# Output projection as seven block products instead of plain tiles, with the first MLP pairs reordered, in a one-core decoder layer

## The chip, the cores and the metric

One Trainium2 chip, one core. The metric is the device time of one execution in microseconds. A profile is one profiled execution; its span runs from the first to the last instruction. The engines are TensorE (PE, with its weight loads PEld), VectorE (DVE), ScalarE (ACT), GpSimd (POOL) and SyncE (SP), which issues the DMAs.

## What is computed

One layer of a hybrid decoder, x of 1024 positions by 1024 features, float32. The part around the change:

```python
merged = (jax.nn.sigmoid(g_a) * (y_att @ w_oa[l])
          + jax.nn.sigmoid(g_b) * (y_sgu @ w_ob[l]))
x = x + merged @ w_out[l]
x = x + conv_gated_mlp(rmsnorm(x, ffn_norm[l]), w_up[l], conv_w[l], conv_b[l], w_down[l])
```

The gates g_a and g_b are columns of an input projection of the normed x; y_att is a sliding-window attention, y_sgu a chunked spatial gating unit. The MLP projects up to twice 2816 columns (22 pairs of a gate tile and a value tile of 128 columns), convolves each over three positions, multiplies silu(gate) with value, and projects down.

## The kernel before

Everything is transposed: features on the 128 partitions, positions along the free axis. TensorE runs in a reduced float format (fp32r), so every operand is split into a high part (ACT, `copy_hi`, line 87) and a low part (the difference, on POOL or DVE), and a product is three matmuls: high by high, high by low, low by high (`mm3`, lines 89 to 93).

The big products of the gates, the up projection and the down projection are already done as seven block products instead of eight: both operands are cut into 2 x 2 blocks, and with A for weights, B for the right side, S and T for sums of their blocks,

```
M1 = A11 B11   M2 = A12 B21   M3 = S4 B22   M4 = A22 T4   M5 = S1 T1   M6 = S2 T2   M7 = S3 T3
```

are combined into the four result blocks. `Blocks.prod` (line 1028) is one such product for one column tile: 4 blocks of 128 x 3 = 12 matmuls of 128x128 by 128x512. The sums of the weights (S) are made ahead for the up projection: `sums_load` and `sums_step` load a unit into one of two `ls` buffers, DVE makes two differences, and the unit goes back to DRAM. `sums_step` is called from `gate_pair` (twice for c > 1) and from the branches.

Stages, in order: attention, the spatial gating unit, the gates (8 `gate_pair`s of 7 products), the branches (16 jobs of 24 matmuls: one tile of y_att or y_sgu products, times 1 + tanh of its gate), the output projection, the up projection (22 pairs), the down projection.

Branches and output projection are **jobs**. `run_jobs` takes them in order: a job's matmuls, then the weight load of the job four ahead, then the weight split of the job two ahead, then the rest of the job (what is done with its result). Weights are loaded into three raw buffers and split into two high (`wh`) and two low (`wl`) buffers. The order in which instructions are issued in the text is the order on every engine (manual schedule), DMAs on SP included.

The output projection before is eight jobs (`out_tile`, in the order D_ORDER) of 8 x 2 x 3 = 48 matmuls: one tile of 128 features over all 1024 positions, in a PSUM tile of two banks. Behind each, DVE adds half of it to x (line 1285), scales by the norm's weight and by the first norm's row factor to h (line 1287), x goes to DRAM, and h is split into the blocks B11, T1, B21, B22, T3 of the up projection, while T2 and T4 stay raw (`raw2`, `raw4`) until `first_pair`. Squares for the second norm are summed in `sq2` (lines 1304 to 1307).

PSUM has eight banks of 128x512 floats: two pools, psA and psC, of two tiles of two banks each. `PS` hands out their tiles in turn.

`first_pair` is the first pair of the up projection: zg with halves g0 and g1, zv with halves v0 and v1. Its products in order: A11·B11 into v1, A12·B21 into g0, S1·T1 into g1, S3·T3 into v0, S4·B22 into g1, S2·T2 into v1, the norm's column sums (`ssq_cols`, line 1354), A22·T4 into v0. The copies between them move a half to SBUF (x1, x7, u2). `fast_pair` does the others; for the second pair it has `rms`, which brings the row factor onto all partitions (line 138) and scales the first pair.

Of the kernel before, what the change touches and what calls it, by code (L numbers as in the profile page):

```python
# [41 lines left out]
def body(ctx, tc, nc, a):  # L42
# [654 lines left out]
    def job_load(i):  # L697
        if i < len(jobs):
            src, nk, _ = jobs[i]
            job_w[i] = wload(src, "wj", nk) if nk else first_left()  # L700
            if not nk:
                next(job_w[i])

    def job_split(i):
        if i < len(jobs):
            nk = jobs[i][1]
            if nk:
                job_w[i] = wsplit(job_w[i], "wj", nk)
            else:
                for _ in job_w[i]:  # L710
                    pass
# [107 lines left out]
    def v_end():  # L819
# [14 lines left out]
        psC = psum["C"].__enter__()  # L834
# [93 lines left out]
    class Left:  # L928
# [75 lines left out]
        def split_r(self, n=0):  # L1004
            if "AX" not in pools:
                pools["AX"] = Y("AX")
# [43 lines left out]
    sums = {"load": 0, "make": 0}  # L1050

    def sums_load():

        i = sums["load"]
        if i < NPAIR:
            x = pools["ls"].tile([128, 3, 4, 128], F, tag="ls", name=nm("ls"), bufs=2)
            nc.sync.dma_start(x[:, 0], a["wup"][2 * i][:, 0:4])
            nc.sync.dma_start(x[:, 1:3], a["wup"][2 * i + 1].rearrange("p (b k) m -> p b k m", b=2))
            sums[i] = x
            sums["load"] += 1  # L1060

    def sums_step():

        i = sums["make"]
        if i < NPAIR:
            sums_load()
            x = sums.pop(i)
            sub(nc.vector, x[:, 0], x[:, 0], x[:, 1])
            sub(nc.vector, x[:, 1], x[:, 1], x[:, 2], ALU.add)
            t = pools["dr"].tile([128, 2, 4, 128], F, tag=f"sum{i}", name=f"sum{i}")  # L1070
            nc.sync.dma_start(t, x[:, 0:2])
            pools.setdefault("sum", {})[i] = t
# [22 lines left out]
    def gates_close():  # L1095
# [3 lines left out]
        pools["mg_cm"] = tc.tile_pool(name="mg", bufs=1)  # L1099
        pools["mg"] = pools["mg_cm"].__enter__()  # L1100

    def gate_pair(c, prev):
# [16 lines left out]
        if c > 1:  # L1119
            sums_step()  # L1120
# [15 lines left out]
        if c > 1:  # L1136
            sums_step()
# [14 lines left out]
        gate_out(("a", c), q.zv)  # L1152
        q.prod(q.g1, "S4", "B22", more=True)
# [35 lines left out]
    B_ORDER = [(br, c + e) for c in range(0, 8, 2) for br in "ba" for e in (0, 1)]  # L1189
    ms = {}  # L1190
# [655 lines left out]
```

## Time and profile before

| | |
|---|---|
| median of 3 runs | 1194.13 us (1193.82 to 1194.5) |
| the profiled execution | 1193.8 us, span 1192.1 us, granted clock 1.0 |
| PE busy | 1180.0 us, 99% of the span, 5890 matmuls |
| DVE, ACT, POOL busy | 877.8, 541.8, 567.4 us |
| DMA queue of the core | 190.26 MB, 45.9% of 16 engines |
| branches | about 380 to 467.6 us of the span |
| output projection | 467.6 to 555 us |
| first MLP pair | from 555 us |

How to read the rows that follow: a group of instructions has its line, engine, operation, out<-in by the program's names, partitions x elements, a count, then busy us and mean ns of one, then the idle time of that engine ahead of them and what ended it. A row of the timeline begins with start and length in us. A row of the waits has who waited for whom, us in total, times, and the longest. A row of a stretch has for each engine its busy us and in brackets the instructions, then the granted PE clock, the DMA share and GB/s.

### The profile page before, as it was taken

What the parts mean: (1) busy time and instruction counts of PE and PEld (TensorE: products, weight loads), DVE (VectorE), ACT (ScalarE), POOL (GpSimd) and SP (SyncE); (2) the same over time, 40 slices, a digit from 0 to 9 for tenths busy, and PEclk for the clock granted to TensorE, in tenths of its full rate; (3) what the DMA queues carried; (4) which work ended last, traced back from release to release, by engine and by line L of the source; (5) the groups of instructions that cost most, each with busy time, mean ns of one, the idle gap of its engine ahead of it and who ended that gap; (6) DMA issues with size and microseconds to landing.
All of it is one profiled execution on the core that took longest, in us unless ns stands there. A gap on an engine that the chain in (4) does not pass through costs nothing.

```text
span 1192.1 us, 15888 instructions
## 1 busy us (share of the span) xinstructions
PE 1180.0 (99%) x5890; PEld 1000.9 (84%) x5890; DVE 877.8 (74%) x1028; ACT 541.8 (45%) x832; POOL 567.4 (48%) x364
## 2 busy tenths in 40 slices
PE   8999999999999999999999999999999999999998
PEld 8989989988888888888888888888888888888887
DVE  7798975745638565668897788878788798865674
ACT  8555567644335222234544444444444445434331
POOL 2367685487768222343756575656657551000000
PEclk9999999999999999999999999999999999999999
DMA  7110133037786997342143342423333258966471
GB/s 272 35 54 19 54 136 130 5 130 260 245 315 212 347 327 278 125 165 100 54 142 108 104 143 98 148 91 124 108 131 124 89 209 290 373 230 194 151 233 67
DMA packets 79134, 191.27 MB, mean 160 GB/s; under 512 B 8913, under 2 KB 9169, under 8 KB 79057
## 3 DMA queue, kind: packets, MB, share of 16 engines
q1 hardware_dynamic: 79056, 190.26, 45.9%
q8 instruction: 46, 0.75, 0.3%
q14 instruction: 32, 0.25, 0.1%
HBM read 139.63 MB, written 50.59 MB: 160 GB/s over the span
## 4 chain that ended last, share of the span: by engine, by line
PE 89%; DVE 4%; POOL 1%; issue 1%; ACT 0%; POOLq 0%; DVEq 0%; ACTq 0%
PE pz L1028 48%; PE pd L1672 10%; PE pdy L1672 8%; PE px L93 2%; PE px L92 2%; PE po L93 2%; PE po L92 2%; PE po L91 2%; PE px L91 2%; PE pvs L91 1%; PE pvs L92 1%; PE pvs L93 1%; DVE ya L529 1%; PE pq L91 1%; PE pq L93 1%; PE pq L92 1%
## 5 line engine op out<-in xcount | busy, mean ns | idle before, releaser
L1028 PE MATMUL pz<-T,qh 128*128 128x512 f32 x472 | 145.6, 390 | 0.0
L988 POOL TENSOR_TENSOR pl<-lp,ph 128x1024 fp32r<-128x1024 f32 x30 | 72.5, 2418 | 83.5 <-ACT ph L87 83.3
L1028 PE MATMUL pz<-B,ph 128*128 128x512 f32 x352 | 109.1, 391 | 0.0
L1028 PEld LDWEIGHTS pz<-T,qh 128*128 128x128 f32 x472 | 88.5, 188 | 18.6 <-ACT u L879 0.3
L1028 PE MATMUL pz<-T,ql 128*128 128x512 f32 x236 | 91.8, 389 | 0.0
L108 POOL TENSOR_TENSOR wjl<-wj,wjh 128x512 fp32r<-128x512 f32 (+1 forms) x24 | 40.6, 1692 | 95.8 <-ACT wjh L87 95.8
L988 POOL TENSOR_TENSOR ql<-lq,qh 128x1024 fp32r<-128x1024 f32 x30 | 76.9, 2565 | 9.1 <-ACT qh L87 9.1
L1028 PEld LDWEIGHTS pz<-B,ph 128*128 128x128 f32 x352 | 65.3, 188 | 15.0 <-ACT x L1519 1.8
L1044 DVE TENSOR_TENSOR pz<-pz,rstd_b 128x1024 f32<-128x1024 f32 x60 | 73.9, 1232 | 4.2 <-ACT rstd_b L141 2.1
L988 POOL TENSOR_TENSOR s3l<-s,s3h 128x512 fp32r<-128x512 f32 x29 | 39.8, 1373 | 69.7 <-ACT s3h L87 69.7
L1028 PE MATMUL pz<-T,s3h 128*128 128x512 f32 x232 | 71.4, 389 | 0.0
L1028 PE MATMUL pz<-B,pl 128*128 128x512 f32 x176 | 68.6, 390 | 0.0
L1672 PE MATMUL pd<-bl,ah 128*128 128x512 f32 x176 | 68.5, 389 | 0.0
L1672 PE MATMUL pd<-bh,ah 128*128 128x512 f32 x176 | 68.5, 389 | 0.0
L1672 PE MATMUL pd<-bh,al 128*128 128x512 f32 x176 | 68.5, 389 | 0.0
L1028 PE MATMUL pz<-T,AX 128*128 128x512 f32 x264 | 63.4, 389 | 0.0
L1028 PE MATMUL pz<-B,AX 128*128 128x512 f32 x264 | 63.4, 389 | 0.0
L1028 PEld LDWEIGHTS pz<-T,AX 128*128 128x128 f32 x264 | 49.6, 188 | 10.3
L1028 PEld LDWEIGHTS pz<-B,AX 128*128 128x128 f32 x264 | 49.6, 188 | 10.3
L1378 DVE SCALAR_TENSOR_TENSOR tg<-pz,cp,tg 128x1023 f32<-128x1023 f32 (+1 forms) x44 | 56.2, 1278 | 0.8
L1378 DVE SCALAR_TENSOR_TENSOR tv<-pz,cp,tv 128x1023 f32<-128x1023 f32 (+1 forms) x44 | 56.2, 1277 | 0.8
L988 POOL TENSOR_TENSOR AX<-lr,AX 128x1024 fp32r<-128x1024 f32 x22 | 53.7, 2440 | 5.1 <-ACT AX L87 5.1
(342 smaller groups left out, 3511.8 us busy)
## 6 DMA issues: line engine op xcount, KB each, us to landing
ls<-wup SPq DMA_DIRECT2D x22, 512.0 KB, 5.3
sum<-ls SPq DMA_DIRECT2D x22, 512.0 KB, 5.3
lp<-wup SPq DMA_DIRECT2D x22, 512.0 KB, 3.6
ra<-wdown SPq DMA_DIRECT2D x44, 256.0 KB, 4.6
b<-T SPq DMA_DIRECT2D x44, 256.0 KB, 3.8
B<-tv SPq DMA_DIRECT2D x33, 256.0 KB, 2.0
T<-tt SPq DMA_DIRECT2D x33, 256.0 KB, 2.0
b<-B SPq DMA_DIRECT2D x33, 256.0 KB, 3.1
```

The source lines that it names most:

```text
L91: nc.tensor.matmul(out, wh, mh, start=first, stop=False, **kw)
L92: nc.tensor.matmul(out, wh, ml, start=False, stop=False, **kw)
L93: nc.tensor.matmul(out, wl, mh, start=False, stop=last, **kw)
L108: nc.gpsimd.tensor_tensor(l[:, :nk, :], r[:, :nk, :], h[:, :nk, :].bitcast(F), op=ALU.subtract)
L529: nc.vector.tensor_tensor(ya[r, 2 * half:2 * half + 2, b * 128:(b + 1) * 128], p[r, g], o[r], op=ALU.add)
L988: nc.gpsimd.tensor_tensor(l, r, h.bitcast(F), op=ALU.subtract)
L1028: nc.tensor.matmul(o, p[:, k, :], y[:, q, k, :], start=not more and k == 0 and j == 0, stop=k == 3 and j == 2, skip_group_check=True)
L1044: nc.vector.tensor_tensor(z, z, rstd_b, op=ALU.mult)
L1378: nc.vector.scalar_tensor_tensor(t[:, j:], p[:, 0:1024 - j], cw[:, ci, 2 - j:3 - j], t[:, j:], op0=ALU.mult, op1=ALU.add)
L1672: nc.tensor.matmul(o[d], p[:, k - k0, m], q[:, k - k0, :], start=new and k == 0 and j == 0, stop=k == HK - 1 and j == 2, skip_group_check= ...
```

## The change

The output projection becomes fourteen jobs (`out_group`), two for each of seven block products, 24 matmuls each (4 tiles d x 2 blocks k x 3). merged is kept raw in `mraw`, and its sums T are formed in place: three differences in `m_done` as the branches end, the rest and the splits in `m_prep`, two groups ahead. The sums of w_out come from eight new units of `sums_step` (four DVE operations each), in DRAM as `d_so`; `gate_pair` calls `sums_step` three times instead of two (twice for c = 1). The branches' order pairs tile c with c + 4.

The eight PSUM banks hold X (four halves, psC) and Yb (four halves, psA) through the whole projection. M1 goes to X, is copied to Yb (`copies`), M2 onto Yb gives C11; M6 onto X, M7 into Yb, M5 onto X gives C22, M3 onto X gives C12, M4 onto Yb gives C21. Each end (`end_c11` and so on) adds half the block to x, stores it, and makes the up projection's blocks with h = x times the norm's weight alone; the row factor is now applied in `rms` whole. Each end yields ahead of its last quarter, d = 3, and there `run_jobs` puts the weight split of the job two ahead.

`first_pair` takes PSUM tiles from psC and runs A11·B11 into v1, S3·T3 into v0, S1·T1 into g1, A12·B21 into g0, S4·B22 into g1, S2·T2 into v1, A22·T4 into v0. The squares of C21 and C12 are added within it. The norm's column sums move into the second pair, where the products now go A11·B11, column sums, A12·B21, row factors, S1·T1, S3·T3.

The diff, cut to what matters (`first_left` also changes its form, and `job_load`, `job_split` call functions kept in the job):

```diff
@@ run_jobs
             m = jobs[i][2](job_w.pop(i))
             next(m)
             job_load(i + 4)
+            if len(jobs[i]) > 3:
+                next(m)
             job_split(i + 2)
             for _ in m:
                 pass
@@ sums
+    UNITS = [("o", 0), ("o", 1)]
+    for c in range(6):
+        UNITS += [("u", 2 * c), ("o", c + 2), ("u", 2 * c + 1)]
+    UNITS += [("u", i) for i in range(12, NPAIR)]
...
+            else:
+                sub(nc.vector, x[:, 3], x[:, 2], x[:, 3], ALU.add)
+                sub(nc.vector, x[:, 2], x[:, 0], x[:, 2])
+                sub(nc.vector, x[:, 0], x[:, 3], x[:, 0])
+                sub(nc.vector, x[:, 1], x[:, 1], x[:, 0])
+                nc.sync.dma_start(d_so[i // 2][:, :, 256 * (i % 2):256 * (i % 2) + 256], x)
@@ gate_pair
-        if c > 1:
-            sums_step()
+        sums_step()
...
         gate_out(("a", c), q.zv)
+        if c > 1:
+            sums_step()
         q.prod(q.g1, "S4", "B22", more=True)
@@ branch, merged
-    B_ORDER = [(br, c + e) for c in range(0, 8, 2) for br in "ba" for e in (0, 1)]
+    B_ORDER = [(br, c + e) for c in range(4) for br in "ba" for e in (0, 4)]
...
+    def m_done(c):
+        k, m = c % 4, mraw[c // 4]
+        m_split("B11" if c < 4 else "B21", k, m[:, k, L])
+        if c >= 4:
+            m0 = mraw[0]
+            sub(nc.vector, m0[:, k, H], m[:, k, H], m0[:, k, H])
+            sub(nc.vector, m0[:, k, L], m0[:, k, H], m0[:, k, L], ALU.add)
+            sub(nc.vector, m[:, k, L], m[:, k, L], m0[:, k, L])
+    def m_prep(g):
+        n, ks = OUT[g // 2][1], slice(2 * (g % 2), 2 * (g % 2) + 2)
+        if n in ("B11", "B21"):
+            return
+        src = mraw[n in ("B22", "T4")][:, ks, L if n in ("T2", "T4") else H]
+        if n == "T1":
+            sub(nc.vector, src, mraw[1][:, ks, H], mraw[0][:, ks, L])
+        m_split(n, ks, src)
@@ out_tile and last_tile go, in their place
+    OUT = (("M1", "B11", 0), ("M2", "B21", 1), ("M6", "T2", 0), ("M7", "T3", 2), ("M5", "T1", 3), ("M3", "B22", 1),
+           ("M4", "T4", 3))
...
+    def sq_add(n, d, tmp):
+        c = (L, H)[int(n[2]) - 1]
+        sq2 = pools["sq2"][:, c]
+        nc.scalar.activation(tmp, acs[n][:, d, :], AF.Square)
+        nc.vector.tensor_tensor(sq2, sq2, tmp, op=ALU.add)
...
+    def end_c11():
+        t = acs["C11"]
+        for d in range(4):
+            if d == 3:
+                yield
+            half_add(Yb[d], Yb[d], t[:, d, :])
+            nc.scalar.copy(t[:, d, :], Yb[d])
+            x2_store("C11", d)
+            hi("B11", d, Yb[d], gain(d))
+            if d:
+                lo_gain("B11", d - 1, Yb[d - 1], gain(d - 1))
+        lo_gain("B11", 3, Yb[3], gain(3))
...
+    def end_c12():
+        t, h11, h22 = acs["C12"], acs["C11"], acs["C22"]
...
+        def late(d):
+            lo("T1", d, X[d])
+            nc.vector.tensor_tensor(tr[:, 1, d, :], h22[:, d, :], X[d], op=ALU.subtract)
+            hi("T3", d, tr[:, 0, d, :])
+            hi("T2", d, tr[:, 1, d, :])
+        for d in range(4):
+            if d == 3:
+                yield
+                lefts[0].sums_r()
+                lefts[0].split_p()
+            half_add(X[d], X[d], t[:, d, :])
+            nc.scalar.copy(t[:, d, :], X[d])
+            x2_store("C12", d)
+            nc.vector.scalar_tensor_tensor(tr[:, 0, d, :], X[d], pools["ng2"][:, d:d + 1], h22[:, d, :],
+                                           op0=ALU.mult, op1=ALU.add)
+            nc.vector.scalar_tensor_tensor(X[d], X[d], gain(d), h11[:, d, :], op0=ALU.mult, op1=ALU.subtract)
+            hi("T1", d, X[d])
+            if d:
+                late(d - 1)
+        late(3)
+    def end_c21():
+        t, tr = acs["C21"], traw[0]
+        def late(d):
+            lo_gain("B21", d, Yb[d], gain(4 + d))
+            nc.vector.scalar_tensor_tensor(Yb[d], Yb[d], gain(4 + d), tr[:, 1, d, :], op0=ALU.mult, op1=ALU.subtract)
+            hi("T4", d, Yb[d])
+        for d in range(4):
+            if d == 3:
+                yield
+                lefts[0].split_q()
+                lefts[0].split_r(0)
+                for i in range(4):
+                    lo("T2", i, tr[:, 1, i, :], nc.gpsimd)
+            half_add(Yb[d], Yb[d], t[:, d, :])
+            nc.scalar.copy(t[:, d, :], Yb[d])
+            x2_store("C21", d)
+            hi("B21", d, Yb[d], gain(4 + d))
+            if d:
+                late(d - 1)
...
+        def main(w):
...
+            for d in range(4):
+                for k in range(2):
+                    for j, (p, q) in enumerate(((0, 0), (0, 1), (1, 0))):
+                        nc.tensor.matmul(o[d], w[p][:, k, 128 * d:128 * d + 128], y[:, q, 2 * kp + k, :], ...)
+            yield
...
+            if g + 2 < 14:
+                m_prep(g + 2)
+            if g == 6:
+                scaled("C11", 0)
+            if g == 10:
+                lefts[0].split_s3()
+                scaled("C22", 4)
+            ends = {1: copies, 3: end_c11, 9: end_c22, 11: end_c12, 13: end_c21}
+            if g in ends:
+                yield from ends[g]()
+            else:
+                yield
...
+            if g == 12:
+                for d in range(4):
+                    lo("T3", d, traw[0][:, 0, d, :], nc.gpsimd)
@@ first_pair
         q.prod(q.v1, "A11", "B11")
         nc.scalar.copy(x1, q.v1)
         nx.load_p()
+        q.prod(q.v0, "S3", "T3")
+        nc.scalar.copy(x7, q.v0)
...
         q.prod(q.g1, "S1", "T1")
+        nc.scalar.copy(u5, q.g1)
+        nc.vector.tensor_tensor(x7, x7, q.g1, op=ALU.add)
+        q.prod(q.g0, "A12", "B21")
+        nc.vector.tensor_tensor(q.g0, x1, q.g0, op=ALU.add)
         nx.split_p()
         nx.split_s3()
+        for d in range(4):
+            sq_add("C21", d, Yb[d])
+        for d in range(4):
+            sq_add("C12", d, Yb[d])
         q.prod(q.g1, "S4", "B22", more=True)
         q.prod(q.v1, "S2", "T2", more=True)
+        nc.scalar.copy(u2, q.v1)
+        nc.vector.tensor_tensor(q.v1, x7, q.v1, op=ALU.add)
...
         q.prod(q.v0, "A22", "T4", more=True)
@@ fast_pair, second pair
         if rms:
-            rms()
+            rms(0)
+            q.prod(q.g0, "A12", "B21", more=True)
+            rms(1)
...
             prev.tap_v()
-            q.prod(q.g0, "A12", "B21", more=True)
+            q.prod(q.g1, "S1", "T1")
```

More of the change, by code (lines that the diff above doesn't have):

```diff
@@ L698, in job_load @@
         if i < len(jobs):
[L699 to L702, printed above, removed]
+            job_w[i] = jobs[i][0]()
     def job_split(i):
         if i < len(jobs):
[L706 to L711, printed above, removed]
+            job_w[i] = jobs[i][1](job_w[i])
     def run_jobs():
@@ L1345, in body @@
-    late = {}
-    for i in range(8):
-        out_tile(i)
+                ac_load("C11")
+            o = Yb if s in ("M2", "M7", "M4") else X
+            y = rt[n]
+            for d in range(4):
+                for k in range(2):
+                    for j, (p, q) in enumerate(((0, 0), (0, 1), (1, 0))):
+                        nc.tensor.matmul(o[d], w[p][:, k, 128 * d:128 * d + 128], y[:, q, 2 * kp + k, :],
+                                         start=s in ("M1", "M7") and kp == 0 and k == 0 and j == 0,
+                                         stop=kp == 1 and k == 1 and j == 2, skip_group_check=True)
```

309 lines of the change are left out of this document (150 added, 159 removed).

## The prediction

> **What bounds the kernel now.** I read the page first, then busy time by stretch, then the chain that ended last in order of time, then the groups of instructions around the change.
>
> ```profile
> span 1192.1 us, 15888 instructions
> ...
> PE 1180.0 (99%) x5890; PEld 1000.9 (84%) x5890; DVE 877.8 (74%) x1028; ACT 541.8 (45%) x832; POOL 567.4 (48%) x364
> ```
>
> TensorE is busy for all but 12 us of the span. By stretch (microseconds busy of PE, PEld, DVE, ACT, POOL; the first row is the last of the branch products, the next two are the output projection, the fourth the first MLP pair):
>
> ```profile
> 424.00:467.60 43.60, 43.60 (x194) 36.09 (x193) 27.56 (x27) 9.73 (x12) 11.57 (x8) 1.00 0.84 303
> 467.60:511.00 43.40, 43.40 (x193) 35.97 (x192) 25.36 (x21) 12.29 (x15) 14.74 (x8) 1.00 0.41 148
> 511.00:555.00 44.00, 44.00 (x196) 36.45 (x195) 35.37 (x30) 14.49 (x20) 17.25 (x9) 1.00 0.37 135
> 555.00:581.00 26.00, 26.00 (x132) 22.06 (x132) 20.97 (x22) 14.21 (x21) 16.66 (x8) 1.00 0.28 91
> ```
>
> PE never stops in any of the four, and ACT works a third of the time. The chain (start, length, what) says the same: from 554.98 on it is one run of matmuls.
>
> ```profile
> 554.98 16.33 PE pz L1028 x72
> 571.32 1.68 PE pz L1354 x16
> 573.00 5.61 PE pz L1028 x24
> 578.60 1.78 PE pz L138 x16
> ```
>
> 72 matmuls in 16.33 us: **0.227 us each**. So a matmul taken out is worth 0.227 us, and any wait that PE meets is paid in full. Everything hangs on whether the side engines still keep ahead of PE.
>
> **What is removed.** The projection is 8 tiles x 48 = 384 matmuls; seven products of two groups x 24 are 336. 48 x 0.227 = **-10.9 us**. The old tiles' DVE work on h goes too; PE never waited for it, so it counts nothing. Adding and squaring stay.
>
> **What I count at nothing.** In the branches DVE gains three 0.69 us differences per second-half tile, some 8 us over the stage, and the lows shrink; DVE was busy 27.6 of 43.6 us there. SP gains 20 weight issues, 8 row loads and 8 stores of about 0.33 us; the DMA share in the projection was 0.4, and three buffers let a load run two groups ahead. Should a load come late all the same, PE pays it in full.
>
> **What the new groups need.** A group is 24 x 0.227 = 5.46 us of PE, half an old tile, with the same weight work. The rows for one instruction:
>
> ```profile
> L108 POOL TENSOR_TENSOR wjl<-wj,wjh 128x1024 fp32r<-128x1024 f32 x8 | 19.2, 2395 | 39.4 <-ACT wjh L87 39.4
> L1225 DVE TENSOR_TENSOR ml<-m,mh 128x1024 fp32r<-128x1024 f32 x8 | 9.8, 1225 | 9.1 <-ACT mh L87 9.1
> L87 ACT ACTIVATE wjh<-wj 128x1024 fp32r<-128x1024 f32 x8 | 8.5, 1062 | 25.5 <-issue 11.1 <-PE po L92 6.5 <-PE px L92 6.5
> L87 ACT ACTIVATE B<-h 128x512 fp32r<-128x512 f32 x12 | 7.3, 628 | 30.8 <-DVE h L1287 25.1 <-DVE h L1327 5.7
> L1264 POOL TENSOR_TENSOR T<-h,T 128x512 fp32r<-128x512 f32 x3 | 3.9, 1295 | 4.4 <-ACT T L87 4.4
> L1326 DVE SCALAR_TENSOR_TENSOR ac<-px,ac 128x512 f32<-128x512 f32 x2 | 1.4, 683 | 0.0
> L1038 ACT COPY u<-pz 128x512 f32<-128x512 f32 x2 | 1.2, 588 | 3.8 <-DVE pz L1037 3.8
> ```
>
> The split of group g+2 takes the buffers of group g, so it starts when group g ends: ACT 1.06, then POOL 2.40, with hops 3.6 us, as here (start, length; 489.5 is the end of a tile):
>
> ```profile
> 489.56 1.06 ACT L87 ACTIVATE wjh<-wj 128x1024 fp32r<-128x1024 f32 x1 [1.90 <-issue]
> 489.74 1.22 DVE L1285 SCALAR_TENSOR_TENSOR ac<-px,ac 128x1024 f32<-128x1024 f32 x1 [3.70 <-PE px L93]
> 490.70 2.39 POOL L108 TENSOR_TENSOR wjl<-wj,wjh 128x1024 fp32r<-128x1024 f32 x1 [2.62 <-ACT wjh L87]
> 490.99 0.33 SPq L1288 DMA_DIRECT2D x<-ac  x1
> 491.00 3.17 DVE L1287 SCALAR_TENSOR_TENSOR h<-ac,cp,rstd_b 128x1024 f32<-128x1024 f32 x1
> 494.21 1.16 ACT L87 ACTIVATE B<-h 128x512 fp32r<-128x512 f32 x2 [3.58 <-DVE h L1287]
> ```
>
> The low part is wanted by the group's third matmul, 5.46 + 0.45 us after the end of group g. **Slack: 2.3 us.** In the text a group issues m_prep and all of its end but the last quarter ahead of the split, and each engine takes its work in that order. Two more things are seen here. A DVE operation with two SBUF inputs stands still while POOL runs: h started at 491.00, POOL ended at 493.09, and h took 3.17 instead of about 1.1. And two readers of one PSUM tile on different engines follow one another:
>
> ```profile
> DVE x L885 <- ACT x L884: 4.5, 1, 4.5
> ```
>
> Both only read the tile pe, yet DVE waited 4.5 us for ACT. The changed program orders every access to one tile (two banks) so.
>
> I now lay these durations end to end, engine by engine, from the start of group 0 (time 0; back-to-back 512s step by 0.55 on ACT, 0.6 to 0.7 on DVE).
>
> Group 3 (end of C11). POOL splits group 4 until 20.0, so the low part of T2 holds DVE until 21.1, 2 us after the first half of Yb is ready. Then add, copy, hi (0.68 + 0.59 + 0.6) alternate between DVE and ACT for three quarters; the split of group 5 starts at 27.3 instead of 21.9, POOL ends at 30.9, wanted at 27.75: **3.2 us**. The squares and splits behind it give 1.2 at group 6; T1's difference and the four scalings ahead of the split, 0.5 at group 8. Group 10 waits for the adds that read X: 0.6. POOL's three sums of squares and DVE's lows, which stop for POOL, give 2.3 at group 11 and 2.4 at group 12.
>
> Group 11 (end of C12) is the worst. DVE comes free at 73.75. Each quarter is add 0.68, copy 0.59, two operations 1.35, hi 0.6, and the next add on that tile waits for the hi: 3.3 us, twice; then low and difference of the first quarter 1.4, the third quarter's add, copy and two 2.7, low and difference 1.4, hi 0.6. The split of group 13 starts 12.5 us on, at 86.3, and POOL ends at 89.8; wanted at 81.65: **8.2 us**.
>
> Sum in the projection: 3.2 + 1.2 + 0.5 + 0.6 + 2.3 + 2.4 + 8.2 = **+18.4 us**. From below, group 13's chain alone, started with all else done, still costs 5.9, and group 5's about 2: 8. Above: 24.
>
> **First pair.** Group 13 ends at 94.9, A11·B11 (12 x 0.227 = 2.73) at 97.6. S3·T3 writes v0, in the tile of v1, and so waits for the copy of v1 into x1. That copy stands on ACT behind all of end_c21: two quarters of add, copy, hi, with the lows, T4 differences and their hi woven in, then split_q and split_r (2.1 on ACT), then two quarters more. From 93.55 I count to 109.2: **11.6 us** of idle PE. Counted only from the third quarter's add, as if all ahead were done, it is 8.2. In before the product behind A11·B11 went to the other tile. Then A12·B21 waits for x7+g1 in its tile (1.7), S4·B22 for x1+g0 (1.0), and A22·T4 for v1's last sum, which now stands behind eight square-and-add pairs that share tiles (0.6 + 0.7 each way, 11.2 us from the end of A12·B21 against 6.5 of PE work): 4.7. Sum **+19.0** (13 to 22). In the second pair S1·T1 moves ahead of S3·T3, and the x7 copy sits behind both taps: **+1.3** (0 to 2). POOL's lows of T3 and T2 (8 x 1.3) end before those waits do.
>
> **Clock.** At the head PE waited and then ran slowly:
>
> ```profile
> 6.25 0.58 PE L91 MATMUL pkv<-wkv,x 128*128 128x256 f32 x1 [1.85 <-ACT x L87]
> ...
> 8.81 0.41 PE L91 MATMUL pkv<-wkv,x 128*128 128x256 f32 x1
> 9.02 0.41 PE L92 MATMUL pkv<-wkv,x 128*128 128x256 f32 x1
> ...
> 11.01 0.28 PE L91 MATMUL pkv<-wkv,x 128*128 128x256 f32 x1
> 11.13 0.28 PE L92 MATMUL pkv<-wkv,x 128*128 128x256 f32 x1
> ```
>
> A step of 0.21 us until about 10.5, then 0.12: some 4 us at near half pace, about 2 us lost. After the gaps of 8 and 11 us I expect the same; the first is partly covered by the waiting behind it: **+3** (0 to 6). The Trainium skill, page "TensorE: Matmul & The Clock Gate", Part 1, has it as a rule that a window of about 3.4 us without work halves the clock until a window of work has passed; by it the 4.7 us gap would cost too, and the sum would be about 1.5 us higher.
>
> **Gates.** Three sum steps a pair instead of two (eight new units, each 512 KB in and out). The queue held a load back for a landed store:
>
> ```profile
> SPq L1057 <- DMA sum<-ls: 38.2, 6, 8.1
> ```
>
> ```profile
> ls<-wup SPq DMA_DIRECT2D x12, 512.0 KB, 5.6
> ...
> sum<-ls SPq DMA_DIRECT2D x11, 512.0 KB, 6.2
> ```
>
> A unit in one of two buffers is load 5.6, two subtractions about 1.8, store 6.2: 6.8 us per unit, 20.4 for three, against 7 x 2.73 = 19.1 of PE. DVE would slip about 1.3 us a pair, 8 over six pairs, and S4·B22 bears 5.4 us of lateness of x7. Loads with less beside them land sooner. From 0 to 12; I take **+2**, near the free end, as PE did not wait here before.
>
> **Sum.** -10.9 + 18.4 + 19.0 + 1.3 + 3 + 2 = +32.8 on the profiled execution's 1193.8 (span 1192.1 plus 1.7): 1226.6. The median of the runs is 0.3 higher: **1227 us**.
>
> **Rivals.** (a) *The side engines keep pace.* If the split of group 13 starts within 2.4 us of the end of group 11 and the C21 work within the products ahead of S4·B22, the matmuls saved show: 1193.8 - 10.9 plus up to 6 of small waits, 1183 to 1189. For it: ACT is idle two thirds of the stage before. Against: the alternation, not the load, sets the chain. (b) *Only the projection pays*: v0 and v1 are different banks, and if PE may write the one while the other waits for its copy, S3·T3 follows at once and the later waits mostly fall inside the products: 1193.8 - 10.9 + 18.4 + 3 = 1204. For it: PE had no wait in this stage before. Against: L885's wait, and the order of ACT. The Trainium skill, page "PSUM — Partial Sum Buffer", section "PSUM bank collisions raise a hardware error", asks for engines to be kept apart bank by bank; by that rule alone (b) would be the outcome, 23 us below the forecast. (c) *The gates are bound too*: ten more, 1237.
>
> Chances: forecast 0.62, (a) 0.07, (b) 0.15, (c) 0.15, no change 0.01. The range reaches from the lower ends (-10.9 + 8 + 13 + 2 = 1206) to 1242, with (c) and the upper ends of the clock; it leaves out (a) and part of (b). A measurement tells 0.2% (2.4 us) from no change: faster 0.07, same 0.01, slower 0.92.
>
> **What would show it.** PE's waits: 3 us before group 5 and 8 before group 13 for the low part of the weights, some 11 before S3·T3 for ACT's x1, 4 to 5 before A22·T4 for DVE. PE's matmuls should number 48 fewer, and its busy time with them. I am wrong if PE runs through the fourteen groups, if S3·T3 follows A11·B11 at once, or if the gates lose more than a few microseconds.

## The result, and the profile after

The changed kernel takes **1277.28 us** (median of 6 runs, 1273.85 to 1279.75) against 1193.97 us of the kernel before (6 runs, 1193.18 to 1194.5): a ratio of **1.0694, interval 1.0676 to 1.0712**. The forecast was 1227, in a range of 1206 to 1242: the sign was right, the size was not. The profiled execution took 1278.34 us, with a span of 1276.6.

The top of the page of after, with the row of the granted clock in 40 slices:

```profile
span 1276.6 us, 16055 instructions
...
PE 1199.7 (94%) x5842; PEld 1005.7 (79%) x5842; DVE 922.0 (72%) x1094; ACT 568.7 (45%) x883; POOL 588.3 (46%) x375
...
PEclk9999999999899899997789999999999999999999
```

PE issues the 48 matmuls less that were counted (5842 against 5890), and yet is busy 20 us longer: many of them ran at a lower clock. Where the time went is read by stretch. First before, from 268 us, where the two kernels still run alike, to the branches, the projection and the first MLP pair (columns as in the prediction; the third number from the end is the granted clock):

```profile
268.00:380.70 112.70, 112.70 (x498) 93.31 (x497) 65.67 (x66) 49.46 (x60) 84.08 (x46) 1.00 0.77 263
380.70:467.80 87.10, 87.10 (x386) 72.12 (x386) 54.13 (x55) 19.86 (x25) 28.14 (x18) 1.00 0.85 309
467.80:554.80 87.00, 87.00 (x385) 72.08 (x384) 60.41 (x51) 26.74 (x34) 31.99 (x17) 1.00 0.39 142
```

And after, the same three stages with their longer bounds, and the first pair:

```profile
268.00:412.90 144.90, 121.64 (x494) 97.32 (x493) 87.74 (x90) 49.68 (x61) 84.17 (x46) 0.94 0.72 242
412.90:507.20 94.30, 89.70 (x386) 73.31 (x385) 68.24 (x69) 16.55 (x26) 28.42 (x18) 0.96 0.84 300
507.20:612.60 105.40, 87.83 (x338) 68.72 (x336) 63.02 (x68) 54.28 (x78) 46.69 (x23) 0.89 0.43 145
612.60:680.00 67.40, 50.11 (x207) 39.87 (x206) 31.99 (x40) 26.56 (x40) 34.29 (x21) 0.87 0.16 55
```

Length less busy time is what PE waited; length times (1 - clock) is about what the low clock took (the last row's waits are those up to 680 us).

| stage | longer by | PE's waits | low clock | products |
|---|---|---|---|---|
| gates, to the branches | 32.2 | 23.3 | 8.7 | |
| branches | 7.2 | 4.6 | 3.8 | |
| projection | 18.4 | 17.6 | 11.6 | -10.9 |
| first pair to the end | 26.7 | 17.3 | 8.8 | |
| **sum** | **84.5** | **62.8** | **32.9** | **-10.9** |

The three right-hand sums give 84.8, the span's growth is 84.5, so no large term is missing. The low clock's 32.9 is a little too much, as some of it falls into the waits: PE was busy 1199.7 us with 10.9 us of products less than the 1180.0 of before, so the low clock took 30.6. The waits of PE in after (who waited for whom, us in total, times, longest) name the places:

```profile
PE pz L1022 <- ACT x L1124: 20.1, 6, 4.8
PE px L1450 <- ACT woh L87: 10.5, 3, 6.6
PE pz L1022 <- ACT tmp L1579: 9.7, 1, 9.7
PE px L1450 <- POOL wol L1434: 6.7, 5, 1.9
PE po L91 <- ACT wjh L87: 4.5, 1, 4.5
PE pz L1022 <- DVE pz L1599: 4.4, 1, 4.4
PE pz L1022 <- DVE x L1142: 2.1, 1, 2.1
...
PE pz L1022 <- DVE tmp L1587: 1.4, 1, 1.4
```

Rows two and four are the projection's weight splits (17.2), three, six and the last the first pair; all of these were forecast. The first row wasn't: six waits in `gate_pair` for the copy of x1, 1.5 to 4.8 us, one in each of the pairs 2 to 7 (row seven stands in the gates too, row five in the branches). One of the six, with what stands ahead of it on ACT:

```profile
339.05 0.59 ACT L1032 COPY u<-pz 128x512 f32<-128x512 f32 x1 [8.89 <-DVE pz L1031]
342.40 1.02 ACT L1095 ACTIVATE th<-pz 128x1024 f32<-128x1024 f32 x1 [2.76 <-DVE pz L1038]
343.32 0.58 ACT L1124 COPY x<-pz 128x512 f32<-128x512 f32 x1
343.95 0.95 PE L1022 MATMUL pz<-x,ph 128*128 128x512 f32 x2 [3.93 <-ACT x L1124]
```

ACT copies u2, then makes the tanh, then copies x1; the first two wait for VectorE's sums of the pair ahead, and those stand on VectorE behind a w_out unit that ends at 338.4.

### The profile page after: what moved, and what is told of

It is laid out like the page before. It is cut to its first block, busy times and chain, and to the rows that moved or that the text cites. A ratio compares the mean times of both kernels' runs of the same rounds, so it can differ in the third digit from the quotient of the medians.

```text
span 1276.6 us, 16055 instructions
## 1 busy us (share of the span) xinstructions
PE 1199.7 (94%) x5842; PEld 1005.7 (79%) x5842; DVE 922.0 (72%) x1094; ACT 568.7 (45%) x883; POOL 588.3 (46%) x375
## 4 chain that ended last, share of the span: by engine, by line
PE 63%; DVE 13%; DMA 6%; issue 6%; ACT 5%; POOL 4%; SPq 0%; ACTq 0%; POOLq 0%; DVEq 0%
PE pz L1022 32%; PE pd L1794 9%; PE pdy L1794 7%; DVE ls L620 3%; PE px L1450 3%; DMA ls<-wout 3%; DMA sum<-ls 2%; PE po L93 2%; PE po L91 2%; PE po L92 2%; POOL wol L1434 1%; DVE xa L620 1%; DVE pz L1038 1%; PE pu L93 1%; PE pu L91 1%
## 5 line engine op out<-in xcount | busy, mean ns | idle before, releaser
L1022 PE MATMUL pz<-T,qh 128*128 128x512 f32 x472 | 148.3, 396 | 5.4 <-DVE pz L1599 4.4
L620 DVE TENSOR_TENSOR ls<-ls 128x512 f32<-128x512 f32 (+1 forms) x76 | 81.4, 1071 | 58.5 <-DMA ls<-wup 29.8
L1022 PE MATMUL pz<-x,ph 128*128 128x512 f32 x128 | 45.6, 441 | 20.1 <-ACT x L1124 20.1
L1434 POOL TENSOR_TENSOR wol<-wo,woh 128x1024 fp32r<-128x1024 f32 x14 | 34.5, 2465 | 55.9 <-ACT woh L87 55.9
L1022 PEld LDWEIGHTS pz<-T,s3h 128*128 128x128 f32 x232 | 44.5, 193 | 19.4 <-ACT tmp L1579 10.1
```

The lines of the kernel that those rows point to most:

```text
L620: eng.tensor_tensor(out, x, y, op=op)
L1022: nc.tensor.matmul(o, p[:, k, :], y[:, q, k, :], start=not more and k == 0 and j == 0, stop=k == 3 and j == 2, skip_group_check=True)
L1434: nc.gpsimd.tensor_tensor(l, r, h.bitcast(F), op=ALU.subtract)
```

## The experiments

Eighteen runs, each timed against the kernel before on the same chip. "Branches from" is the first branch product in the run's profile; kernels with the same gates differ there by up to 4 us.

| run | what | median us | ratio to before | branches from | clock |
|---|---|---|---|---|---|
| before | | 1193.97 | | 380.7 | 1.000 |
| after | | 1277.28 | 1.0694 [1.0676, 1.0712] | 412.9 | 0.974 |
| e1 | no w_out units | 1236.04 | 1.0367 [1.0348, 1.0387] | 380.6 | 0.981 |
| e2 | units alone, on before | 1233.75 | 1.0337 [1.0322, 1.0352] | 414.0 | 0.988 |
| e3 | weight splits first | 1285.51 | 1.0775 [1.0759, 1.0791] | 409.5 | 0.968 |
| e4 | x1 inside the end | 1269.4 | 1.0650 [1.0633, 1.0668] | 410.4 | 0.980 |
| e5 | units without subtractions | 1247.72 | 1.0460 [1.0444, 1.0475] | 389.5 | 0.982 |
| e6 | unit third in a pair | 1260.66 | 1.0569 [1.0553, 1.0585] | 399.8 | 0.981 |
| e7 | single waits, on before | 1241.67 | 1.0408 [1.0386, 1.0430] | | 0.981 |
| e8 | e1 + e4 | 1230.86 | 1.0323 [1.0306, 1.0340] | 379.3 | 0.987 |
| e9 | half units, four buffers | 1335.67 | 1.1181 [1.1163, 1.1199] | 438.2 | 0.960 |
| e10 | subtractions alone | 1251.52 | 1.0486 [1.0470, 1.0501] | 387.7 | 0.982 |
| e11 | e6 + e4 | 1256.5 | 1.0524 [1.0507, 1.0542] | 403.6 | 0.981 |
| e12 | split of group 13 first | 1273.66 | 1.0674 [1.0658, 1.0690] | 411.1 | 0.977 |
| e13 | unit on GpSimd | 1276.75 | 1.0695 [1.0677, 1.0712] | 419.8 | 0.977 |
| e14 | e6 on GpSimd | 1263.99 | 1.0587 [1.0571, 1.0603] | 407.4 | 0.979 |
| e15 | e14 + e4 | 1258.51 | 1.0547 [1.0525, 1.0568] | 405.7 | 0.980 |
| e16 | own buffer | 1276.78 | 1.0708 [1.0675, 1.0741] | 410.5 | 0.981 |
| e17 | e16 + e6 + e4 | 1256.87 | 1.0534 [1.0518, 1.0549] | 400.4 | 0.978 |
| e18 | tanh stored by ACT | 1268.2 | 1.0639 [1.0621, 1.0657] | 403.6 | 0.979 |

### What lengthens the gates: e1 and e2

**e1**, on after:

```diff
-    UNITS = [("o", 0), ("o", 1)]
-    for c in range(6):
-        UNITS += [("u", 2 * c), ("o", c + 2), ("u", 2 * c + 1)]
-    UNITS += [("u", i) for i in range(12, NPAIR)]
+    UNITS = [("u", i) for i in range(NPAIR)]
```

Not shown: the third call of `sums_step` goes too, and the projection reads plain blocks of w_out.

> The kernel after, without the eight units that form the sums of w_out in the gates: two sums steps per pair from c = 2 on, as before; the projection reads plain blocks of w_out where it read the sums (that part of the computation is left out). Theory G (the units are what made the gates longer, 32 us at the start of the branches against the 2 us forecast): the branches start at 381 to 384 again instead of 412.7, and the time falls by 28 to 36, to 1241 to 1249. Rival W (the gates lengthen by the low clock and by something else of the change, and the waits of projection and first pair carry the loss): the branches still start after 400, and the time stays above 1265.

**e2**, on before: after's `sums` code and third call of `sums_step`, and nothing else.

> The kernel before, with nothing but the eight units of w_out's sums and the third sums step added to the gates (from a copy of w_out in the block layout; the sums are stored and not read). Theory G: what the units cost needs nothing else of the change, so the branches start at 410 to 414 instead of 380.5, and the time is 1194 + 28 to 36 = 1222 to 1230. Rival W: the units alone cost what was forecast, +2 (0 to 12): the time is 1194 to 1206.

Both answer for theory G: 41.2 us less without the units, and 40.6 more with them alone, both some 4 to 5 beyond what was expected. The gates of e1 are again those of before, at a full clock; its projection still has its loss:

```profile
268.00:380.60 112.60, 112.60 (x499) 93.23 (x498) 65.13 (x66) 49.15 (x60) 84.71 (x46) 1.00 0.78 264
...
467.60:574.50 106.90, 89.13 (x337) 69.75 (x336) 64.19 (x69) 54.34 (x78) 46.70 (x23) 0.87 0.43 143
```

The largest waits of PE in e2 are the new ones of after, to 0.2 us, in a kernel whose projection and MLP are untouched:

```profile
PE pz L1028 <- ACT x L1132: 20.3, 6, 4.8
PE po L91 <- ACT wjh L87: 4.4, 1, 4.4
```

So half of the loss has nothing to do with the seven products themselves: it is the price of making w_out's sums in the gates.

### What a wait costs in clock: e7

**e7**, on before:

```diff
+COPIES = {4: 6, 6: 7, 8: 8, 10: 9, 12: 10, 14: 12, 16: 14, 18: 18}
...
-        nc.scalar.copy(x1, q.g0)
+        for _ in range(COPIES.get(n, 1)):
+            nc.scalar.copy(x1, q.g0)
```

> The kernel before, with the copy of x1 in eight of the MLP pairs made 6, 7, 8, 9, 10, 12, 14 and 18 times over (same values again), so that PE waits before A12.B21 some 0.6 us longer for each further copy, in a stage where the clock is otherwise 1.00. Theory C (the low clock after is the answer to single waits of PE of a few us, whatever the stage): pairs with waits of 4 us and more are followed by a clock under 0.95 in the next 20 us, and waits under 2 us by none. Rival N (the low clock comes of many waits close together): after each of these single waits the clock stays at 1.00. The time itself: 1194 + 25 of waits + 0 to 15 of clock.

Theory C holds. The time came out above what was expected because the waits sum to 34.3 us and not 25; the clock's part is at the upper end of its range, as PE's busy time shows (1180.0 in before, for the same 5890 matmuls):

```profile
PE 1195.2 (96%) x5890; PEld 1010.7 (81%) x5890; DVE 884.8 (71%) x1028; ACT 587.4 (47%) x908; POOL 566.1 (46%) x364
```

That is 15.2 us, and with the waits it makes up the 49.8 by which the span grew. Five of the eight waits, asked for by window:

```profile
PE pz L1029 <- ACT x L1521: 1.7, 1, 1.7
PE pz L1029 <- ACT x L1521: 2.7, 1, 2.7
PE pz L1029 <- ACT x L1521: 3.5, 1, 3.5
PE pz L1029 <- ACT x L1521: 6.9, 1, 6.9
PE pz L1029 <- ACT x L1521: 9.3, 1, 9.3
```

And the 14 us from the end of each on, in the same order (PE's matmuls are the first number in brackets, the clock is third from the end):

```profile
683.72:697.72 14.00, 14.00 (x62) 11.59 (x63) 11.00 (x10) 6.77 (x8) 9.35 (x5) 1.00 0.29 98
724.80:738.80 14.00, 14.00 (x55) 11.45 (x56) 10.57 (x9) 6.63 (x8) 9.04 (x5) 0.88 0.25 93
811.23:825.23 14.00, 14.00 (x50) 11.29 (x51) 9.42 (x9) 6.14 (x7) 8.38 (x5) 0.79 0.22 83
904.33:918.33 14.00, 14.00 (x52) 11.37 (x53) 10.96 (x8) 6.21 (x7) 8.86 (x5) 0.83 0.20 76
954.27:968.27 14.00, 14.00 (x49) 11.31 (x50) 9.24 (x8) 6.14 (x7) 8.28 (x5) 0.78 0.22 82
```

Behind the wait of 1.7 us the clock is full and PE gets through 62 matmuls. Behind the others it gets through 55, 50, 52 and 49; at 0.227 us for one, that is 1.6, 2.7, 2.3 and 3.0 us lost. The waits of 2.5, 2.9 and 4.8 us, not shown, lost 1.8, 1.6 and 2.0. So the price hardly grows beyond a wait of 3.5 us: behind the longest wait the clock was already at 0.50 over its last 4 us, where it costs nothing. The mean clock of the whole run, 0.981, would put the loss at 23.6 us and is no measure of it.

The Trainium skill, page "TensorE: Matmul & The Clock Gate", Part 1, lets the clock go to half after an idle window of about 3.4 us; here single waits of 2.5 and 2.7 us already paid, so the measurement decides. After has about a dozen waits of 2 us and more; its 30.6 us are some 2.6 for each, within these prices. The length of a wait alone doesn't decide: in after a wait of 2.3 us in the gates left the clock at 1.00 (62 matmuls in the 14 us behind it), and one of 1.9 us in the projection was followed by 0.75 over 6.9 us. Why is not shown.

### Inside the gates: e5, e10, e6, e9

**e5**, on after: the four subtractions of a w_out unit deleted.

> The kernel after, with the eight units of w_out loaded and stored again but without their four subtractions (the sums of w_out are left out). Theory D (the pair is bound by the loop of the two buffers: load lands, VectorE, store lands, next load; 24 us for three units, of which VectorE's work on the w_out unit is the smaller part): the loop loses about 5 us of VectorE per pair, so the branches start at 392 to 403 instead of 412.7 (380.5 before), and the time falls by 12 to 25, to 1252 to 1265. Rival V (VectorE's four subtractions in front of the pair's own sums are the whole cost): the branches start before 386, and the time is that without the units, 1236 to 1243.

**e10**, on e1: four subtractions of 128x256 put where the unit stood in the pairs 2 to 7 (six of the eight units), no transfers.

> The kernel after without the units of w_out (their sums are left out, plain blocks read instead), but with VectorE's four subtractions of 128x256 in the second step of the pairs 2 to 7, on a part of w_up's unit that isn't stored, and w_up's units in the first and third step: VectorE's work of the units without their transfers. The transfers without the work cost 1247.7 - 1236.0 = 11.7 us, both together 41.2. Theory D (each alone fits under a pair's products, only the two in one loop do not): the branches start at 381 to 387 and the time is 1236 to 1246. If the two parts add up: 1236 + 29.5 x 6/8 = 1258, 1253 to 1265. Rival V: as the sum, with the branches at 396 or later.

The transfers alone cost 1247.7 - 1236.0 = 11.7, the subtractions alone (six units of eight) 15.5, both 41.2. Neither theory has it: each part costs by itself, and together they cost 14 more than their sum. Part of the 14 may be VectorE's own: in e10 the four subtractions took 3.6 us in four of the six pairs, less than in after. e5 fell by more than theory D allowed.

**e6**, on after:

```diff
-        UNITS += [("u", 2 * c), ("o", c + 2), ("u", 2 * c + 1)]
+        UNITS += [("u", 2 * c), ("u", 2 * c + 1), ("o", c + 2)]
```

> The kernel after, with the unit of w_out in the third step of a pair, behind the pair's sums on VectorE, and the two units of w_up in the first and second. The same loads, subtractions and stores. Theory D (the loop of two buffers, wherever the units stand): the branches start at 408 to 416, the time is within 6 of 1277. Rival V (the unit's place ahead of the sums on VectorE is the cost): the branches start before 397, and the time falls by 16 or more, below 1261.

The order alone is worth 16.6 us, as rival V had it, with the branches 3 us later than it asked. The trace says why. A w_out unit on VectorE in after (start, length):

```profile
331.52 6.84 DVE L620 TENSOR_TENSOR ls<-ls 128x256 f32<-128x256 f32 x4 [4.31 <-DMA ls<-wout]
```

Beside it on GpSimd in after:

```profile
331.38 1.30 POOL L982 TENSOR_TENSOR s3l<-s,s3h 128x512 fp32r<-128x512 f32 x1
332.62 1.48 POOL L620 TENSOR_TENSOR lr<-lq,lp 128x512 f32<-128x512 f32 x1
334.18 1.36 POOL L620 TENSOR_TENSOR lr<-lp,lr 128x512 f32<-128x512 f32 x1
335.51 2.57 POOL L982 TENSOR_TENSOR ql<-lq,qh 128x1024 fp32r<-128x1024 f32 x1
```

The same four instructions in e6, in the third place, where GpSimd rests from 333.2 to 336.3:

```profile
333.63 1.79 DVE L620 TENSOR_TENSOR ls<-ls 128x256 f32<-128x256 f32 x4
```

Four subtractions, four operations of GpSimd: each of VectorE's takes until 0.3 us behind the end of one of GpSimd's. In the pairs 2 to 7 the unit takes 4.9 to 9.6 us in after, 1.8 to 2.6 in e6. The Trainium skill, page "SBUF — State Buffer", section "SBUF: two separate sides", calls the port that the two share an exclusive lock held for a whole instruction; 6.84 against 1.79 us agrees. The price is thus by instruction more than by size, as single units of e9 show.

**e9**, on after: each unit in two halves (`[128, 3, 2, 128]` and `[128, 4, 128]` in place of `[128, 3, 4, 128]` and `[128, 4, 256]`), `bufs=4` in place of 2, two halves to a step, three loads ahead.

> The kernel after, with each unit of the sums made in two halves, through four buffers of half the size instead of two: the same memory, bytes and sums, twice as many transfers and VectorE instructions at half the length, three loads ahead instead of one. Theory D (what binds a pair is the loop load, VectorE, store, next load through two buffers): with four halves on the way the loop takes some 12 us for four halves, 18 to 19 us for the six of a pair, so the branches start at 383 to 396 instead of 412.7, and the time falls by 18 to 38, to 1239 to 1259. Rival V (VectorE's work in front of the pair's sums sets it, whatever the buffers): the branches start at 405 or later and the time is within 8 of 1277.

It is the worst of all, 58 us slower than after, against both theories. Two of its half units on VectorE, the first while GpSimd rests:

```profile
338.21 1.27 DVE L620 TENSOR_TENSOR ls<-ls 128x128 f32<-128x128 f32 x4 [2.57 <-DMA ls<-wout]
344.10 5.80 DVE L620 TENSOR_TENSOR ls<-ls 128x128 f32<-128x128 f32 x4 [4.61 <-DMA ls<-wout]
```

Half the size takes 5.80 us beside a working GpSimd, where the whole took 6.84. That is not what makes e9 slow, though: the two halves together take 7.1 us, about as long as the whole. What grew are SP's waits for landed stores ahead of the units' loads, 99.3 us from 250 us to the branches against 61.3 in after. PE's largest waits there are for the next pair's weights, 20.2 us in four; their split stands on GpSimd behind a sum that waits for a load which SP issues behind those of the units. That this is the whole of it no run shows.

### Which hop closes the loop: e13, e14, e16, e18

**e13**, on after, and **e14**, on e6: `nc.vector` becomes `nc.gpsimd` in the unit's four subtractions.

> The kernel after, with the four subtractions of each w_out unit given to GpSimd, in the second place of a pair as in after; loads, stores and buffers stay. Theory S (the unit is long because each of its VectorE instructions has to let a GpSimd operation finish, 6.8 us against 1.8 us where GpSimd rests): VectorE's part goes as it went with no subtractions at all, GpSimd has room, and the time is near that run's: branches at 388 to 398, 1246 to 1258. Rival D (the loop of the buffers binds, and it doesn't matter who subtracts): branches at 405 or later, 1268 or more; GpSimd, which takes its work in order, would then also hold the weight splits behind the unit's load.

> The kernel after, with the w_out unit in the third place of a pair and its subtractions on GpSimd, where GpSimd otherwise rests for some 7 us. Theory S: VectorE already did this unit in 1.8 us in the third place, so little is left to gain from moving it: within 5 of 1260.7. Rival D2 (in the third place the units of w_up, behind one another in the first and second, are what waits, and any change of the third is hidden): the same number, so this run tells only against a large further gain, which would be 1250 or less.

Nothing is gained by e13 (1276.75), as rival D had it, though VectorE is rid of the work. The wait has moved: SP's store now waits longer, for GpSimd's subtractions, and the weights of the next pair, behind it in SP's order, come later. (In after the store waited 27.9 us for VectorE, and GpSimd 28.1 for that load.) From the waits of SP's queue and of GpSimd in e13, up to 420 us:

```profile
SPq L1084 <- POOL ls L620: 44.5, 8, 8.1
```

```profile
POOL s L620 <- DMA lq<-wga: 39.4, 5, 12.9
```

In the third place (e14) GpSimd does it as well as VectorE, within 4 us. **e16**, on after:

```diff
-                x = pools["ls"].tile([128, 4, 256], F, tag="ls", name=nm("ls"), bufs=2)
+                x = pools["ls"].tile([128, 4, 256], F, tag="lo" if i != 1 else "ls", name=nm("lo"), bufs=1 if i != 1 else 2)
```

with two tanh buffers in place of three, and `th_load` of branch n + 2 behind the use of branch n's.

> The kernel after, with a buffer of their own for the w_out units (all but the second), in memory taken from the tanh's staging (two buffers instead of three; the branches load their tanh one product later), so that the load of a w_out unit needn't wait for the landing of a w_up store. VectorE's work and its place, all transfers and the queue stay. Theory D (the loop store, landing, load, subtractions binds a pair, 25 us): without that hop a pair needs VectorE's 16 to 18 us, under the 19.1 of its products, so the branches start at 381 to 394 and the time falls by 20 to 38, to 1239 to 1257. Rival V (VectorE's stops for GpSimd in front of the sums bind, and the load's wait only fills time that is there): the branches start at 404 or later, the time is above 1265.

Theory D falls in this form: 1276.78, branches from 410.5. Two units on VectorE in e16, a pair apart:

```profile
328.32 6.98 DVE L620 TENSOR_TENSOR lo<-lo 128x256 f32<-128x256 f32 x4 [3.13 <-DMA lo<-wout]
...
352.24 6.98 DVE L620 TENSOR_TENSOR lo<-lo 128x256 f32<-128x256 f32 x4 [3.08 <-DMA lo<-wout]
```

23.9 us, though the load no longer waits for a store: it is issued at 344.3, behind SP's tanh store, and lands 8 us later. Nor did the tanh buffer that was taken away cost anything to speak of: ACT's waits ahead of the tanh are 21.9 us up to the branches, 21.6 in after. **e18**, on after:

```diff
-        nc.sync.dma_start(d, t)
+        nc.scalar.dma_start(d, t)
```

> The kernel after, with the stores of the tanh (two a pair, 512 KB each) issued by ACT, which makes the tanh, and no longer by SP. All work, buffers and VectorE's order stay. Theory Q (the loop of a pair runs through SP's order: sums, tanh, its store on SP, the load behind it, landing, w_out's subtractions): without the wait of SP for the tanh, 2 to 5 us a pair, a pair falls from 24 to 20 or 22 us, the branches start at 394 to 404 and the time falls by 8 to 22, to 1255 to 1269. Rival V (VectorE's 6.8 us for the unit, ahead of the sums, and the waits shaped around it): the branches start at 408 or later, and the time is within 6 of 1277.

The median falls by 9.1, the weak end of theory Q, and the branches begin 9.3 earlier in the profile, which is of its quickest run (1263.4). So SP's order is one hop, VectorE's place another, and no single one closes the loop.

### The projection and the first pair: e3, e12, e4 and the combinations

**e3** takes the two lines `if len(jobs[i]) > 3: next(m)` out of `run_jobs`; **e12** does so for group 11 alone.

> The kernel after, with the split of the weights of group g + 2 issued straight behind the products of group g, ahead of the operations that end a block. Theory P (in the projection PE waits for the weight split because ACT's copy and POOL's difference stand behind the ends): the waits for woh and wol, 10.5 + 6.7 = 17.2 us in the profile after, fall to 3 or less, the low clock behind them goes too, and the time falls by 12 to 20, to 1257 to 1265. Rival Q (the ends, held up by the splits, free the banks and the products of merged later, and PE waits for them instead): the sum of PE's waits in the projection stays above 12, and the time is within 5 of 1277.

> The kernel after, with only the split of group 13's weights put ahead of the end of block C12; group 13 waited 6.6 to 8 us for it. Theory P (one split out of its place is cheap, since the 8.5 us lost with all splits moved came from the other groups): the wait of group 13 falls below 2 and the time falls by 3 to 10, to 1267 to 1274. Rival Q (the split must wait for group 11's last product to free its buffer, and holds the end of C12 behind it on ACT, so the first pair waits for that end instead): PE's waits in the first pair rise by 5 or more, and the time is 1274 to 1284.

e3 is slower than after by 8 us, so rival Q. Its largest waits from 500 to 640 us have none for w_out's weights (`ph` is a weight of the first pair's):

```profile
PE pz L1020 <- ACT tmp L1577: 13.6, 1, 13.6
PE px L1448 <- ACT rT L87: 7.4, 1, 7.4
PE pz L1020 <- ACT ph L87: 7.2, 1, 7.2
PE px L1448 <- DVE ac L1297: 5.8, 1, 5.8
PE px L1448 <- ACT px L1328: 2.1, 1, 2.1
PE px L1448 <- DVE rT L1233: 1.8, 1, 1.8
```

17.2 us of waits for weights became 17.1 for the ends and for merged's splits, and the first pair's grew from 16.3 to 28.6 (the rows on pz here, 1.2 more for A11·B11's weights, and 4.4, 1.4 and 0.8 as in after). In e12 group 13 no longer waits (6.6 and 1.3 in after), but S3·T3's wait for x1 rose from 9.7 to 15.6, and A11·B11 waits 3.2 for its own weights. Both theories had a part: the time is in theory P's range, the first pair's waits rose by 9.1 as rival Q asked, and as the intervals of e12 and after overlap, no gain is shown. With two weight buffers ACT's copy can't start before the group ahead ends, so whatever goes first holds up the other.

**e4** stops the last job behind its products, and `first_pair` drives its end (not shown: `end_c21` also stops ahead of d = 2 and no longer calls `split_q`):

```diff
         q.prod(q.v1, "A11", "B11")
+        tail = pools.pop("tail")
+        next(tail)
         nc.scalar.copy(x1, q.v1)
+        w.split_q()
         nx.load_p()
         q.prod(q.v0, "S3", "T3")
+        next(tail)
         nc.scalar.copy(x7, q.v0)
+        for _ in tail:
+            pass
```

> The kernel after, with A11.B11, x1's copy and the split of S1 and A22 put between the second and the third tile of the last block's end, so that S3.T3 needn't wait for the end. Theory F (the 9.7 us wait of S3.T3 is one of order on ACT alone): that wait falls to under 2, the waits behind it grow by 3 at most, and the time falls by 6 to 14, to 1263 to 1271. Rival E (the end's own length sets it: B21's and T4's low parts are ready no sooner, so A12.B21 and A22.T4 wait instead): PE's waits in the first pair still sum to 12 or more, and the time is within 4 of 1277.

Theory F by the time, which falls by 7.9: of S3·T3's 9.7 us 1.1 are left. But A12·B21's wait grows from 1.4 to 5.8, more than the 3 allowed, so that the first pair's waits, 12.1, stay where rival E had them; the end's own length is part of it. **e8** (e1 and e4), **e11** (e6 and e4), **e15** (e14 and e4), **e17** (e16, e6 and e4):

> The kernel after without the eight units (the sums of w_out are left out, plain blocks read instead) and with A11.B11 and x1's copy put into the last block's end, so that only the projection's own waits and what is left of the first pair's stand against the 10.9 us of products saved. If the two edits add up: 1236 - 8 = 1224 to 1232, some 3% above before, with PE's waits near 38 us in all and 17 of them in the projection. Rival (without the low clock from the gates the rest comes back to a full clock): below 1215.

> The kernel after with both edits that helped and keep all of the work: the w_out unit third in a pair, and A11.B11 with x1's copy inside the last block's end. If they are independent: 1277 - 16.6 - 7.9 = 1252.7, 1248 to 1258, still 4 to 5% above before. Rival (the low clock from the gates and branches is shared, so the gains overlap): above 1260.

> As the run before, with A11.B11 and x1's copy inside the last block's end. By the run with the third place on VectorE and this edit, 1256.5: 1248 to 1260, still slower than before by 4.5 to 5.5%.

> As the run before, with the w_out unit in the third place of a pair (1.8 us on VectorE instead of 6.8) and with A11.B11 and x1's copy inside the last block's end: all of the work of the change, in the best form found. Theory D: the units cost next to nothing, so the run without them and with the same edit, 1230.9, is met within 10: 1229 to 1241. Rival: 1250 or more. Neither reaches before.

e8 lands where adding up put it, e11 and e15 too; e17 does not reach e8, the own buffer being worth nothing. The best versions with all of the work are e11 and e17, 1256.5 and 1256.9, still 5% above before, and even without the units the projection and the first pair lose 3% (e8). No version here beats before.

## Why the prediction missed

- **Products, -10.9:** right; 5842 matmuls.
- **Projection, +18.4 of waits:** 17.6. The cause given, the splits standing behind the ends in ACT's and POOL's order, is borne out by the rows, 17.2 of it for w_out's weights, and by e3, where other waits take their place. At group 13 it is 6.6 for the high part and 1.3 for the low, 7.9 against 8.2, at group 12 4.6 against 2.4, at group 5 2.7 against 3.2, at group 6 nothing against 1.2.
- **First pair, +19.0:** 16.3 (9.7 + 4.4 + 1.4 + 0.8, against 11.6 + 4.7 + 1.7 + 1.0). e4 shows the first to be a matter of ACT's order. So rival (b), that S3·T3 would follow at once, did not come; the wait is put in by the program's order for whole tiles, and whether the banks would allow more no run shows. **Second pair, +1.3:** 1.7.
- **What was counted at nothing, the branches:** 4.6 of waits, nearly all one wait of 4.5 for `wjh` that e2 has too and e1 has not; so it came with the units. How, no run shows.
- **Gates, +2:** the step that failed. It measured 23.3 of waits, 32.2 with their clock; gates and branches together grew by 39.4, and e2 puts the whole of the units at 40.6. Three things were wrong in it. The unit was charged "two subtractions about 1.8": that is w_up's, while w_out's has four, and in the second place of a pair each of them waits for GpSimd; the unit takes 4.9 to 9.6, 6.84 in the one shown. The stop of VectorE for GpSimd was seen in the prediction's own rows, and not applied here. Then "6.8 us per unit", two buffers overlapping perfectly, left out that one pair's steps are in series: subtractions, the pair's own sums, the tanh and its store on SP, the loads behind that, their landing. Last, the reserve of 5.4 us at S4·B22 was the wrong path: PE waits for x1's copy, which stands on ACT behind u2's copy and the tanh, which wait for VectorE behind the unit. The bound of 12 was built on the same three, so it did not hold the truth either; rival (c), ten more, had the right place and a third of the price.
- **Clock, +3:** the other failed step. It priced only the waits of 8 and 11 us. After lost 30.6 us by PE's busy time (32.9 by the table); in e7 each of the seven single waits from 2.5 us on took 1.6 to 3.0 more.

The two failed terms make up the miss: 23.3 + 4.6 forecast as 2, and 32.9 forecast as 3, are 55.8 us too little; the waits in the projection and the first pairs came out 3.8 lower; 1226.6 + 55.8 - 3.8 = 1278.6, against the profiled execution's 1278.3. With 30.6 for the clock the sum is 1276.3, and some 2 us are small waits outside the table's stretches.

What stays open is which single hop closes the loop of a pair. Taking away the subtractions gives back 29.6 us, moving them 16.6, SP's wait for the tanh 9.1, the shared buffer nothing, and no run took two of SP's hops away at once.

## What to carry to other kernels

Work put "beside" a full engine is to be laid out in the order of each queue that it uses, as one chain per turn, and compared with the turn's length: the unit's mean load on VectorE, GpSimd and the queue was well within the pair here, and the chain was not. VectorE's subtractions of two SBUF tiles paid per instruction while GpSimd ran; before making pieces smaller, look whether it can be put where GpSimd rests. And each wait of TensorE of some 2.5 us or more is to be priced with 1.6 to 3 us of low clock on top, as in e7.

## What the hardware showed that was not expected

The clock fell after a single wait of 2.7 us in an otherwise full stage (e7: 0.88 over the next 14 us) and did not after 1.7 us (1.00). A wait of 9.3 us cost hardly more behind it (3.0 us) than one of 3.5 (2.7). By PE's busy time the loss was 15.2 us in e7 for seven waits, and 30.6 in after. Four subtractions of 128x256 took 1.79 us beside a resting GpSimd and 6.84 beside a working one; four of 128x128 took 1.27 and 5.80.
